# Where the memory tokens of a cross attention are loaded and turned: in the merge before w_mix_out instead of inside it

## The chip, the core and the metric

The kernel runs on one core of one Trainium2 chip. The metric is the device time of one execution in microseconds (us). The engines work side by side, each through its own instructions in order: TensorE (PE, with its weight loads as PEld), VectorE (DVE), ScalarE (ACT), GpSimd (POOL) and SyncE (SP). Transfers are issued by SP (the hardware queue) or by POOL (the software queue) and carried out by 16 DMA engines.

## The reference

One decoder block on 256 tokens of 2048 features, all in float32:

```
u = rms_norm(x);  [q k v z B C g_attn g_conv] = u @ w_in
merged = sigmoid(g_attn) * (attention(q, k, v) @ w_attn_proj)
       + sigmoid(g_conv) * (B * conv3(C * z) @ w_conv_proj)
h = x + merged @ w_mix_out
u = rms_norm(h);  mem_n = rms_norm(mem)          # mem: 256 memory tokens of 2048 features
k, v = halves of mem_n @ w_xkv;  q = u @ w_xq    # 4 heads of 128
h = h + softmax(q k^T / sqrt(128)) v @ w_xo
h = h + swiglu(rms_norm(h));  out = rms_norm(h)
```

The change concerns `rms_norm(mem)` and how its result gets into the layout that `mem_n @ w_xkv` needs: features on the 128 partitions, tokens along the free axis.

## The kernel before, in words

Every product keeps float32 accuracy by splitting both operands into a high part (rounded to fp32r) and a low part (the rest) and adding three partial products. Weights come in tiles of 256 rows by 512 columns (512 KB), loaded by SP into `raw` (five buffers). ScalarE casts a tile to `whi` and VectorE subtracts to get `wlo` (three buffers each; `split`, L54 to L56, called from `weights`, L70). `gemm_ft` (L86) makes [features, tokens]: for each weight tile a matmul of 512 columns with `whi` (L96) and one of 256 with `wlo` (L100). `gemm_tf` (L112) makes [tokens, features]: triples of matmuls of 512 columns (L122, L123, L124), where L123 alone reads `wlo`. Between weight tiles a product runs "hooks", pieces of other work given by the row number k0 at which they are traced.

The order: `w_in` in 17 products of 512 columns (the last eight make the two gates; attention runs in their hooks), then the merge (L513 to L535), then `w_mix_out` (L576 to L588), then the cross attention and the feed-forward part. The merge has eight `gemm_ft` products, `w_attn_proj` and `w_conv_proj` in turn for each of four column blocks, of four weight tiles each. What they leave is gated, added and split into MG. `w_mix_out` has four `gemm_tf` products of eight weight tiles each, with MG as the other operand. Its results are added to `h`, which holds a copy of x that POOL loads at L577.

An activation is transposed without TensorE as follows. `stage_in` (L225) loads a block so that partition 32 i + b holds tokens 32 j + b and the i-th quarter of its columns. `feat` (L208) then transposes its 32 x 32 squares on VectorE (L214, into `xt`, two buffers, two 128 x 256 pieces in each) and calls `high_low` (L217), where ScalarE multiplies by the gain (L221) and VectorE makes the low part (L222). Before the change mem is staged as one tile of [128, 8, 512] in the tile pool `cp`, by four POOL transfers of 512 KB in the first two products of `w_mix_out` (L578 to L580). It is turned by eight calls of `mem_feat` in the last two (L582, L583), and its norm is taken from the staged tile by `stage_rms` (L229, called at L587). The result is XM, the operand of `w_xkv`. The residual h is staged per column block by `bounce` (L249): SP writes the block to DRAM (`hd`, L252) and reads it back in the staged layout (`hst`, four transfers, L227). `h_feat` (L570) turns it, traced as hooks of the two products of `w_xkv` that follow.

Each engine's order is written by a planner when the program is built. It runs a model of the machine's time and gives an engine the next instruction that is ready in that model, the earlier traced first; an instruction can so stand well ahead of its place in the program. `keep_in_program_order` pins an instruction behind the one that was traced before it on its engine. A tile needs a free buffer of its pool, and a pool opened in the room of a closed one waits until that one's tiles are no longer used. `ap` and `cp` are such pools: `h` and `mem` lie where the mixer's tiles were, so their loads start when the merge is over.

Of the kernel before, what the change touches and what calls it, by code (L numbers as in the profile page):

```python
# [17 lines left out]
P = 128  # L18
# [23 lines left out]
def hybrid_block(ctx, tc, a, out):  # L42
# [69 lines left out]
    def gemm_tf(W, kt, X, c0, evac, cols=C, hooks=None, last=1, lead=0, head=1):  # L112
        """[tokens, features] tiles of X.T @ W[:, c0:c0+cols]; the first and last weight tiles go token tile by token tile."""
# [50 lines left out]
    # keep the tensor engine's clock up while the first loads are under way  # L164
# [4 lines left out]
    # additive masks: current block keeps key <= query, previous block key > query  # L169
# [11 lines left out]
    def sumsq(src, ss):  # L181
        junk = sp.tile([P, C], F32, tag="junk", name="junk", bufs=1)
        nc.scalar.activation(junk, src, AF.Square, accum_out=ss)
# [14 lines left out]
    # A staged block holds 32 i + b on its partitions, for token 32 j + b and features (i, f):  # L198
    # transposing its 32 x 32 squares puts features on the partitions and tokens next to each other.
# [8 lines left out]
    def feat(stage, m, k0, n, kx, g, X, j0=0, nj=NJ):  # L208
        """X[:, kx + k, 0/1, tokens] = high/low parts of (stage * g) for the features f = m a + k0 + k."""
# [3 lines left out]
        for k in range(n):  # L213
            nc.vector.transpose(xt[:, k, :].rearrange("p (j b) -> p j b", b=Q), v[:, k0 + k, j0:j0 + nj, :])  # L214
# [14 lines left out]
    def stage_rms(stage, name):  # L229
        """1/rms of the tokens of a staged block: [P, NT] by partition, and [P, T] on every partition."""  # L230
# [18 lines left out]
    def bounce(c, st, eng=nc.sync):  # L249
        """Stage column chunk c of h by way of DRAM."""  # L250
# [5 lines left out]
    def spread(r, name):  # L256
        """rB[p, t*P + n] = r[n, t] on every partition p."""
# [12 lines left out]
    # ================= mixer =================  # L270
    with ExitStack() as ph:
        mp = ph.enter_context(tc.tile_pool(name="mp", bufs=1))
        ap_ = ph.enter_context(tc.tile_pool(name="ap", bufs=2))
# [17 lines left out]
        k_sb = mp.tile([P, NT, KVW], F32, tag="k_sb", name="k_sb")  # L291
        v_sb = mp.tile([P, NT, KVW], F32, tag="v_sb", name="v_sb")
# [20 lines left out]
        g_x, g_mem, g_ffn = gain("g_xattn", C // P), gain("g_mem", KD), gain("g_ffn", C // P)  # L313
# [10 lines left out]
        # rotary, in place, on GpSimd  # L324
# [20 lines left out]
        # gated short convolution, [features, tokens]  # L345
        yc = mp.tile([P, KC, 2, T], F32R, tag="yc", name="yc")
        for c in range(CW // C):
            zts = []

            def evac_z(m, p0, p1, zts=zts):  # L350
                if not zts:
                    zts.append(mp.tile([P, C // P, T], F32, tag="zt", name="zt"))
# [8 lines left out]
            def evac_c(m, p0, p1, c=c, zts=zts):  # L361
                zt = zts[0]
                cz = mp.tile([P, T + 2], F32, tag="cz", name="cz", bufs=4)
# [26 lines left out]
        # attention stages per kv head  # L390
        qT = mp.tile([P, NH // 2, T], F32, tag="qT", name="qT")
        kT = mp.tile([P, 2, NKV // 2, T], F32, tag="kT", name="kT")
        ks_sb = mp.tile([P, NT, KVW], F32, tag="ks_sb", name="ks_sb")
# [103 lines left out]
        }  # L497
        i = 0
        for dst, base in ((sa, AW + 2 * KVW + 3 * CW), (sc, AW + 2 * KVW + 3 * CW + D)):
            for c in range(D // C):  # L500
                hooks = {4 * j + 2: [f] for j, f in enumerate(steps.get(i, ()))}
                i += 1

# [9 lines left out]
        # merge  # L513
        MG = xp.tile([P, KD, 2, T], F32R, tag="X", name="MG")
        for c in range(D // C):
# [16 lines left out]
            gemm_ft(rows_kp(a["w_attn_proj"][0]), AW // P, oT, c * C, evac_a)  # L532
            gemm_ft(rows_kp(a["w_conv_proj"][0]), KC, yc, c * C, evac_m)
        while pending:
            next(pending.pop(0), None)  # L535

# [15 lines left out]
    # ================= cross attention =================  # L552
    with ExitStack() as ph:
        cp = ph.enter_context(tc.tile_pool(name="cp", bufs=1))
        cap = ph.enter_context(tc.tile_pool(name="cap", bufs=2))
        mem = cp.tile([P, NJ, C], F32, tag="mem", name="mem")
        xv = a["x"][0].rearrange("(t p) d -> p t d", p=P)

        XM = cp.tile([P, KD, 2, T], F32R, tag="XM", name="XM")
# [4 lines left out]
        rm, hs = [], {}  # L564

# [7 lines left out]
        def mem_feat(k):  # L573
            feat(mem, KD, k, 2, k, g_mem, XM)

        for c in range(D // C):  # L576
            hooks = {4: [lambda: nc.gpsimd.dma_start(h[:, :, c * C:(c + 1) * C], xv[:, :, c * C:(c + 1) * C])]}  # L577
            if c < 2:  # L578
                hooks[8] = [lambda: stage_in(mem, a["mem"][0], 2 * c, eng=nc.gpsimd)]
                hooks[12] = [lambda: stage_in(mem, a["mem"][0], 2 * c + 1, eng=nc.gpsimd)]  # L580
            else:
                for i in range(4):  # L582
                    hooks[2 + 4 * i] = [lambda i=i: mem_feat((c - 2) * KD // 2 + 2 * i)]  # L583
            if c:
                hooks[4].append(lambda: h_stage(c - 1))
            if c == D // C - 1:
                hooks[4].append(lambda: rm.extend(stage_rms(mem, "rmB")))  # L587
# [3 lines left out]
        xs = cp.tile([P, NJ * C], F32, tag="mem", name="xs")  # L591
# [12 lines left out]
        gemm_ft(rows_pk(a["w_xkv"][0], KD), KD, XM, 0, evac_xk, hooks=hooks)  # L604
# [13 lines left out]
        gemm_tf(rows_pk(a["w_xkv"][0], KD), KD, XM, XW, evac_xv(0), cols=HW, hooks=hooks)  # L618
# [168 lines left out]
```

## Time and profile before

| | us |
|---|---|
| median of 3 runs | 1473.47 |
| lowest, highest | 1473.1, 1473.87 |
| span of the profiled execution | 1474.0 |
| TensorE busy in it | 1441.9 |
| VectorE busy | 886.3 |
| ScalarE busy | 724.0 |
| mean granted clock of TensorE | 0.991 |

The profiled execution's own time is its span, 1474.0 us; the profile shows nothing outside it. Positions such as 545.20 are microseconds from the start of the span. Matmuls are pipelined: a duration of 0.39 us is from start to end, and the next one starts 0.23 us after it.

### The profile page before, as it was taken

The numbers are of one execution on the slowest core, as the hardware profiler recorded it, in microseconds if no ns is written. First come the engines' busy times: TensorE is split into PE (matmuls) and PEld (weight loads), VectorE is DVE, ScalarE is ACT, GpSimd is POOL, SyncE is SP. The second block draws the span as 40 slices with busy tenths as digits, with TensorE's granted clock in tenths as the row PEclk, the third lists the DMA queues.
The fourth block names the chain that finished last, engine by engine and source line by source line (L and its number), as shares of the span: only waits on it lengthen the run. The fifth ranks groups of instructions, "written<-read, shape, count | busy, mean of one in ns | idle before, by whom it ended". The sixth has DMA issues, their size and how long they took to land.

```text
span 1474.0 us, 20189 instructions
## 1 busy us (share of the span) xinstructions
PE 1441.9 (98%) x7707; PEld 1227.6 (83%) x7707; DVE 886.3 (60%) x1316; ACT 724.0 (49%) x1115; POOL 46.6 (3%) x67
## 2 busy tenths in 40 slices
PE   7999999999999996999999999999999999999997
PEld 6888888888888875899888888888888888888886
DVE  6557768555557858585655656556556555545454
ACT  6443555554455545565654544545445444434343
POOL 0061000000000010000000000000000000000000
PEclk9999999999999998999999999999999999999999
DMA  8664454456656678865566665665666666555553
GB/s 227 198 188 147 145 170 148 155 176 198 191 176 192 194 204 241 254 192 163 175 186 186 186 195 183 194 188 186 193 190 184 190 193 217 187 188 189 191 188 115
DMA packets 147028, 275.11 MB, mean 187 GB/s; under 512 B 10588, under 2 KB 18804, under 8 KB 146804
## 3 DMA queue, kind: packets, MB, share of 16 engines
q1 hardware_dynamic: 145780, 269.64, 59.3%
q0 software_dynamic: 1152, 4.19, 1.2%
q8 instruction: 60, 0.98, 0.3%
q14 instruction: 36, 0.29, 0.1%
HBM read 269.60 MB, written 4.19 MB: 186 GB/s over the span
## 4 chain that ended last, share of the span: by engine, by line
PE 92%; DMA 2%; POOL 2%; DVE 2%; issue 1%; ACT 0%; ACTq 0%; POOLq 0%; SPq 0%; DVEq 0%
PE acc L96 41%; PE acc L100 21%; PE acc L123 9%; PE acc L124 9%; PE acc L122 9%; DMA mem<-in_mem 2%; DMA x<-in_x 1%; DVE xt L214 1%; PE sps L430 1%; PE ops L483 1%; DVE XM L222 0%; DVE wlo L56 0%; PE tp L472 0%; POOL sa L336 0%; POOL sa L335 0%
## 5 line engine op out<-in xcount | busy, mean ns | idle before, releaser
L56 DVE TENSOR_TENSOR wlo<-raw,whi 128x1024 fp32r<-128x1024 f32 (+1 forms) x506 | 607.0, 1205 | 527.1 <-ACT whi L55 526.9
L55 ACT CAST whi<-raw 128x1024 fp32r<-128x1024 f32 (+1 forms) x506 | 520.2, 1033 | 624.5 <-PE acc L96 359.7
L96 PE MATMUL acc<-X,whi 128*128 128x512 f32 x2368 | 805.8, 396 | 0.0
L100 PE MATMUL acc<-X,wlo 128*128 128x256 f32 x2368 | 607.3, 280 | 0.0
L96 PEld LDWEIGHTS acc<-X,whi 128*128 128x128 f32 x2368 | 435.9, 188 | 83.6 <-issue 0.8
L100 PEld LDWEIGHTS acc<-X,wlo 128*128 128x128 f32 x2368 | 446.2, 188 | 23.9 <-issue 1.1
L124 PE MATMUL acc<-whi,gT 128*128 128x512 f32 x352 | 138.9, 395 | 0.0
L123 PE MATMUL acc<-wlo,gT 128*128 128x512 f32 x352 | 138.9, 394 | 0.0
L122 PE MATMUL acc<-whi,gT 128*128 128x512 f32 x352 | 125.4, 395 | 0.0
L107 ACT COPY half<-acc 128x256 f32<-128x256 f32 x184 | 67.5, 369 | 25.5 <-PE acc L100 23.5
L122 PEld LDWEIGHTS acc<-whi,gT 128*128 128x128 f32 x352 | 66.4, 189 | 15.5
L124 PEld LDWEIGHTS acc<-whi,gT 128*128 128x128 f32 x352 | 66.3, 188 | 15.5
L123 PEld LDWEIGHTS acc<-wlo,gT 128*128 128x128 f32 x352 | 66.3, 188 | 15.4
L123 PE MATMUL acc<-wlo,MG 128*128 128x512 f32 x128 | 51.0, 399 | 12.7 <-DVE wlo L56 12.7
L124 PE MATMUL acc<-whi,MG 128*128 128x512 f32 x128 | 50.6, 395 | 0.0
L122 PE MATMUL acc<-whi,MG 128*128 128x512 f32 x128 | 45.4, 393 | 0.0
L96 PE MATMUL acc<-yc,whi 128*128 128x512 f32 x128 | 43.7, 394 | 0.0
L96 PE MATMUL acc<-oT,whi 128*128 128x512 f32 x128 | 43.5, 394 | 0.0
L122 PE MATMUL acc<-whi,X 128*128 128x512 f32 x96 | 34.4, 401 | 5.9 <-ACT whi L55 3.3
L123 PEld LDWEIGHTS acc<-wlo,MG 128*128 128x128 f32 x128 | 24.5, 192 | 18.7 <-DVE wlo L56 13.5
L123 PE MATMUL acc<-wlo,X 128*128 128x512 f32 x96 | 38.2, 403 | 0.9 <-DVE wlo L56 0.9
L124 PE MATMUL acc<-whi,X 128*128 128x512 f32 x96 | 37.6, 397 | 0.0
(189 smaller groups left out, 1106.1 us busy)
## 6 DMA issues: line engine op xcount, KB each, us to landing
raw<-in_w_ffn_in SPq DMA_DIRECT2D x176, 512.0 KB, 4.3
raw<-in_w_in SPq DMA_DIRECT2D x134, 512.0 KB, 3.8
raw<-in_w_ffn_out SPq DMA_DIRECT2D x88, 512.0 KB, 4.6
raw<-in_w_mix_out SPq DMA_DIRECT2D x32, 512.0 KB, 4.8
raw<-in_w_attn_proj SPq DMA_DIRECT2D x16, 512.0 KB, 4.3
raw<-in_w_conv_proj SPq DMA_DIRECT2D x16, 512.0 KB, 4.0
raw<-in_w_xkv SPq DMA_DIRECT2D x8, 512.0 KB, 3.9
raw<-in_w_xkv SPq DMA_DIRECT2D x16, 256.0 KB, 2.8
```

The costliest lines, as they stand in the source:

```text
L55: nc.scalar.copy(hi, src)
L56: nc.vector.tensor_tensor(out=lo, in0=src, in1=hi.bitcast(F32), op=ALU.subtract)
L96: nc.tensor.matmul(ps[m], lhsT=hi[:, k, ms], rhs=X[:, kk].rearrange("p s t -> p (s t)"), start=(kk == 0), stop=False,)
L100: nc.tensor.matmul(ps[m][:, :T], lhsT=lo[:, k, ms], rhs=X[:, kk, 0, :], start=False, stop=(kk == kt - 1),)
L107: nc.scalar.copy(t2, ps[m][:, T:])
L122: nc.tensor.matmul(o, lhsT=xh, rhs=hi[:, k, :cols], start=(kk == 0), stop=False)
L123: nc.tensor.matmul(o, lhsT=xh, rhs=lo[:, k, :cols], start=False, stop=False)
L124: nc.tensor.matmul(o, lhsT=xl, rhs=hi[:, k, :cols], start=False, stop=(kk == kt - 1))
L214: nc.vector.transpose(xt[:, k, :].rearrange("p (j b) -> p j b", b=Q), v[:, k0 + k, j0:j0 + nj, :])
L430: nc.tensor.matmul(sps[par][:, j].rearrange("p a b -> p (a b)"), lhsT=qT[b:b + 64, hh // 2, t * P:(t + 1) * P], rhs=kT[b:b + 64, sw, kv // ...
L483: nc.tensor.matmul(ops[64 * par:64 * par + 64], lhsT=v_sb[:, kb, vs], rhs=pt[:, t + kb, par::2, :], start=(kb == 0), stop=(kb == t),)
```

## The change

The attention's pool `ap` moves to the right end of the memory and takes in the tiles that only the attention and the convolution use. It is closed before the last gate product, and two pools open in its room: `xm` with XM, and `ms` for staging. Mem is now staged in four column chunks of 512 features, each a tile `mst` of [128, 8, 128] filled by four POOL transfers of 128 KB (512-byte runs). A second copy, in natural layout, comes in eight tiles `mnat` of [128, 512] (256 KB) for the sums of squares. Both have two buffers. Chunks 0 and 1 and natural tiles 0 and 1 are loaded in hooks of the last gate product, the others in the merge. In the merge's first four products (g = 0 to 3) chunk g is turned by two calls of `feat`, whose first transpose is pinned; in each of the eight products one natural tile is squared and summed on ScalarE, pinned as well. The norm comes from these sums (`mem_rms`) with no matmul. Features lie in XM in another order now, so `g_mem` and the rows of `w_xkv` are read in that order too (`rows_pk(..., C // P)`). In `w_mix_out` the loads, the turns and `stage_rms` of mem go. Removed comments and docstrings, and unchanged context, are left out here:

```diff
-    def feat(stage, m, k0, n, kx, g, X, j0=0, nj=NJ):
+    def feat(stage, m, k0, n, kx, g, X, j0=0, nj=NJ, late=False):
         ...
         for k in range(n):
-            nc.vector.transpose(xt[:, k, :].rearrange("p (j b) -> p j b", b=Q), v[:, k0 + k, j0:j0 + nj, :])
+            i = nc.vector.transpose(xt[:, k, :].rearrange("p (j b) -> p j b", b=Q), v[:, k0 + k, j0:j0 + nj, :])
+            if late and not k:
+                tc.keep_in_program_order(i)
...
+    mxp, ms = ExitStack(), ExitStack()
     with ExitStack() as ph:
         mp = ph.enter_context(tc.tile_pool(name="mp", bufs=1))
-        ap_ = ph.enter_context(tc.tile_pool(name="ap", bufs=2))
+        at = ph.enter_context(ExitStack())
+        ap_ = at.enter_context(tc.tile_pool(name="ap", bufs=2, side="right"))
...
         # k_sb, v_sb, zt, cz, qT, kT, ks_sb: from mp to ap_, with the same number of buffers
-        g_x, g_mem, g_ffn = gain("g_xattn", C // P), gain("g_mem", KD), gain("g_ffn", C // P)
+        g_x, g_mem, g_ffn = (gain(n, C // P) for n in ("g_xattn", "g_mem", "g_ffn"))
...
+        mem_in, mem_do = {}, {}
+
+        def mem_open():
+            at.close()
+            xm = mxp.enter_context(tc.tile_pool(name="xm", bufs=1, side="right"))
+            tmp = ms.enter_context(tc.tile_pool(name="ms", bufs=2, side="right"))
+            XM = xm.tile([P, KD, 2, T], F32R, tag="XM", name="XM")
+            ssm = tiny.tile([P, NT, D // C], F32, tag="ssm", name="ssm")
+            mv = a["mem"][0].rearrange("(t p) d -> p t d", p=P)
+
+            def stage(c):
+                mem_in[c] = tmp.tile([P, NJ, P], F32, tag="mst", name="mst")
+                for i in range(P // Q):
+                    stage_in(mem_in[c], a["mem"][0][:, c * C:(c + 1) * C], i, eng=nc.gpsimd)
+
+            def turn(c, k):
+                feat(mem_in[c], C // P, k, 2, c * (C // P) + k, g_mem, XM, late=True)
+
+            def nat(j):
+                mem_in[4 + j] = tmp.tile([P, C], F32, tag="mnat", name="mnat")
+                c, t = j // NT, j % NT
+                nc.gpsimd.dma_start(mem_in[4 + j], mv[:, t, c * C:(c + 1) * C])
+
+            def sums(j):
+                c, t = j // NT, j % NT
+                tc.keep_in_program_order(sumsq(mem_in[4 + j], ssm[:, t, c:c + 1]))
...
                 i += 1
+                if i == 8:
+                    mem_open()
+                    do = mem_do
+                    hooks = {0: [lambda: do["stage"](0)], 2: [lambda: do["stage"](1)],
+                             4: [lambda: do["nat"](0)], 6: [lambda: do["nat"](1)]}
...
+            def mem_hooks(g):
+                hk = {2: [lambda: do["sums"](g)], 4: []}
+                if g < 6:
+                    hk[2].append(lambda: do["nat"](g + 2))
+                if g < 4:
+                    hk[2].append(lambda: do["turn"](g, 0))
+                    hk[4].append(lambda: do["turn"](g, 2))
+                    if g < 2:
+                        hk[4].append(lambda: do["stage"](g + 2))
+                return hk
+
-            gemm_ft(rows_kp(a["w_attn_proj"][0]), AW // P, oT, c * C, evac_a)
-            gemm_ft(rows_kp(a["w_conv_proj"][0]), KC, yc, c * C, evac_m)
+            gemm_ft(rows_kp(a["w_attn_proj"][0]), AW // P, oT, c * C, evac_a, hooks=mem_hooks(2 * c))
+            gemm_ft(rows_kp(a["w_conv_proj"][0]), KC, yc, c * C, evac_m, hooks=mem_hooks(2 * c + 1))
         while pending:
             next(pending.pop(0), None)
+        ms.close()
...
-        mem = cp.tile([P, NJ, C], F32, tag="mem", name="mem")
+        ph.enter_context(mxp)
+        XM = mem_do["XM"]
...
+        def mem_rms():
+            r = rstd_sum(mem_do["ssm"])
+            rm.extend((r, spread(r, "rmB")))
...
-            if c < 2:
-                hooks[8] = [lambda: stage_in(mem, a["mem"][0], 2 * c, eng=nc.gpsimd)]
-                hooks[12] = [lambda: stage_in(mem, a["mem"][0], 2 * c + 1, eng=nc.gpsimd)]
-            else:
-                for i in range(4):
-                    hooks[2 + 4 * i] = [lambda i=i: mem_feat((c - 2) * KD // 2 + 2 * i)]
...
-                hooks[4].append(lambda: rm.extend(stage_rms(mem, "rmB")))
+                hooks[4].append(mem_rms)
...
-        gemm_ft(rows_pk(a["w_xkv"][0], KD), KD, XM, 0, evac_xk, hooks=hooks)
+        gemm_ft(rows_pk(a["w_xkv"][0], C // P), KD, XM, 0, evac_xk, hooks=hooks)
```

## Rows read from the trace of the kernel before

**Rows 1.** The page: TensorE's busy time, and the chain's shares by line.

```profile
PE 1441.9 (98%) x7707; PEld 1227.6 (83%) x7707; DVE 886.3 (60%) x1316; ACT 724.0 (49%) x1115; POOL 46.6 (3%) x67
PE acc L96 41%; PE acc L100 21%; PE acc L123 9%; PE acc L124 9%; PE acc L122 9%; DMA mem<-in_mem 2%; DMA x<-in_x 1%; DVE xt L214 1%; PE sps L430 1%; PE ops L483 1%; DVE XM L222 0%; DVE wlo L56 0%; PE tp L472 0%; POOL sa L336 0%; POOL sa L335 0%
```

**Rows 2.** TensorE's waits, 515 to 650 us: total, times, longest.

```profile
PE acc L123 <- DVE wlo L56: 12.7, 2, 11.5
```

**Rows 3.** VectorE's order of time: start, us, line, out<-in, count, [idle before].

```profile
545.20 0.68 DVE L541 TENSOR_TENSOR h<-acc,h 128x512 f32<-128x512 f32 x1
559.29 2.08 DVE L214 STREAM_TRANSPOSE xt<-mem 128x256 f32<-128x256 f32 x4 [13.41 <-DMA mem<-in_mem]
...
561.87 1.21 DVE L56 TENSOR_TENSOR wlo<-raw,whi 128x1024 fp32r<-128x1024 f32 x1
...
583.98 2.21 DVE L214 STREAM_TRANSPOSE xt<-hst 128x256 f32<-128x256 f32 x4
```

**Rows 4.** TensorE's order of time: merge's start, w_mix_out's start, stop and end.

```profile
433.82 0.39 PE L96 MATMUL acc<-oT,whi 128*128 128x512 f32 x1
...
523.92 0.39 PE L123 MATMUL acc<-wlo,MG 128*128 128x512 f32 x1
...
550.93 0.71 PE L122 MATMUL acc<-whi,MG 128*128 128x512 f32 x2
563.13 0.80 PE L123 MATMUL acc<-wlo,MG 128*128 128x512 f32 x1 [11.49 <-DVE wlo L56]
...
626.20 0.62 PE L96 MATMUL acc<-XM,whi 128*128 128x512 f32 x2
```

**Rows 5.** VectorE's order of time in the third product of w_mix_out.

```profile
591.64 1.22 DVE L56 TENSOR_TENSOR wlo<-raw,whi 128x1024 fp32r<-128x1024 f32 x1 [1.47 <-ACT whi L55]
...
597.08 1.23 DVE L56 TENSOR_TENSOR wlo<-raw,whi 128x1024 fp32r<-128x1024 f32 x1 [1.50 <-ACT whi L55]
```

**Rows 6.** Windows: length, PE, PEld, DVE, ACT, POOL busy, granted clock, DMA, GB/s.

```profile
554.00:556.00 2.00, 0.00 (x0) 0.00 (x0) 0.00 (x0) 0.00 (x0) 0.00 (x0) 1.00 1.04 223
556.00:558.00 2.00, 0.00 (x0) 0.00 (x0) 0.00 (x0) 0.00 (x0) 0.00 (x0) 0.57 1.02 297
...
564.00:566.00 2.00, 2.00 (x6) 1.52 (x6) 2.00 (x5) 0.78 (x2) 0.00 (x0) 0.50 0.88 257
```

**Rows 7.** POOL's order of time, 530 to 626 us: its first instruction there.

```profile
532.01 0.91 POOL L577 DMA_DIRECT2D h<-in_x  x1 [414.06 <-issue]
```

**Rows 8.** DMA queues from 544 to 556 us: packets, MB, share of the engines.

```profile
q0 software_dynamic: 508, 1.85, 65.1%
q1 hardware_dynamic: 506, 0.97, 39.0%
```

**Rows 9.** Windows, the merge's eight products: the third, and the sum of all.

```profile
456.28:467.51 11.23, 11.23 (x66) 9.81 (x65) 10.10 (x21) 6.95 (x12) 0.00 (x0) 1.00 0.59 187
...
sum 89.86, PE 89.86 PEld 78.52 DVE 68.02 ACT 49.23 POOL 0.00; mean PE 11.23 PEld 9.82 DVE 8.50 ACT 6.15 POOL 0.00
```

**Rows 10.** ScalarE's order of time, 540 to 592 us.

```profile
549.80 1.05 ACT L55 CAST whi<-raw 128x1024 fp32r<-128x1024 f32 x1 [5.78 <-DMA raw<-in_w_mix_out]
```

**Rows 11.** DMA issues 530 to 565 (KB, us to landing); hst 585 to 600.

```profile
hd<-h SPq DMA_DIRECT2D x1, 512.0 KB, 4.3
...
DMA to landing us min/median/max: 6.7/7.2/7.5
```

**Rows 12.** VectorE by line, 524 to 626 (busy, mean ns, idle); mem's tile.

```profile
L214 DVE STREAM_TRANSPOSE xt<-mem 128x256 f32<-128x256 f32 x16 | 8.6, 582 | 13.4 <-DMA mem<-in_mem 13.4
L222 DVE SCALAR_TENSOR_TENSOR XM<-xt,g_mem,XM 128x256 fp32r<-128x256 f32 x16 | 6.7, 467 | 0.0
...
DMA to landing us min/median/max: 12.5/18.2/23.8
```

**Rows 13.** VectorE's order of time in the merge's first product.

```profile
439.78 2.36 DVE L56 TENSOR_TENSOR wlo<-raw,whi 128x1024 fp32r<-128x1024 f32 x2 [2.40 <-ACT whi L55]
```

**Rows 14.** The instructions that read pt: duration min/median/max, first and last start.

```profile
L483 PE MATMUL ops<-pt,v_sb x48: 379/379/431, 175.3 to 300.3; 128*64 128x256 f32 x48
```

More of the change, by code (lines that the diff above doesn't have):

```diff
@@ L182, in sumsq @@
         junk = sp.tile([P, C], F32, tag="junk", name="junk", bufs=1)
-        nc.scalar.activation(junk, src, AF.Square, accum_out=ss)
+        return nc.scalar.activation(junk, src, AF.Square, accum_out=ss)
     def rstd_sum(ss):
@@ L290, in hybrid_block @@
         q_sb = mp.tile([P, NT, AW], F32, tag="sc", name="q_sb")
-        k_sb = mp.tile([P, NT, KVW], F32, tag="k_sb", name="k_sb")
-        v_sb = mp.tile([P, NT, KVW], F32, tag="v_sb", name="v_sb")
+        k_sb = ap_.tile([P, NT, KVW], F32, tag="k_sb", name="k_sb", bufs=1)
+        v_sb = ap_.tile([P, NT, KVW], F32, tag="v_sb", name="v_sb", bufs=1)
         def evac_q(c):
@@ L351, in evac_z @@
                 if not zts:
-                    zts.append(mp.tile([P, C // P, T], F32, tag="zt", name="zt"))
+                    zts.append(ap_.tile([P, C // P, T], F32, tag="zt", name="zt", bufs=1))
                 zt = zts[0]
@@ L362, in evac_c @@
                 zt = zts[0]
-                cz = mp.tile([P, T + 2], F32, tag="cz", name="cz", bufs=4)
+                cz = ap_.tile([P, T + 2], F32, tag="cz", name="cz", bufs=4)
                 nc.vector.memset(cz[:, 0:2], 0.0)
@@ L388, in hybrid_block @@
             gemm_ft(W, KD, X1, AW + 2 * KVW + CW + c * C, evac_b)
-        qT = mp.tile([P, NH // 2, T], F32, tag="qT", name="qT")
-        kT = mp.tile([P, 2, NKV // 2, T], F32, tag="kT", name="kT")
-        ks_sb = mp.tile([P, NT, KVW], F32, tag="ks_sb", name="ks_sb")
+        qT = ap_.tile([P, NH // 2, T], F32, tag="qT", name="qT", bufs=1)
+        kT = ap_.tile([P, 2, NKV // 2, T], F32, tag="kT", name="kT", bufs=1)
+        ks_sb = ap_.tile([P, NT, KVW], F32, tag="ks_sb", name="ks_sb", bufs=1)
         oT = mp.tile([P, AW // P, 2, T], F32R, tag="x0", name="oT")
@@ L497, in hybrid_block @@
         }
+        mem_in, mem_do = {}, {}
[19 more added lines that the diff above has]
+                tc.keep_in_program_order(sumsq(mem_in[4 + j], ssm[:, t, c:c + 1]))
+            mem_do.update(stage=stage, turn=turn, nat=nat, sums=sums, XM=XM, ssm=ssm)
         i = 0
@@ L555, in hybrid_block @@
         cap = ph.enter_context(tc.tile_pool(name="cap", bufs=2))
-        mem = cp.tile([P, NJ, C], F32, tag="mem", name="mem")
+        ph.enter_context(mxp)
+        XM = mem_do["XM"]
         xv = a["x"][0].rearrange("(t p) d -> p t d", p=P)
-        XM = cp.tile([P, KD, 2, T], F32R, tag="XM", name="XM")
         X2 = xp.tile([P, KD, 2, T], F32R, tag="X", name="X2")
@@ L571, in h_feat @@
             feat(hs[c], C // P, k, 2, c * (C // P) + k, g, X)
-        def mem_feat(k):
-            feat(mem, KD, k, 2, k, g_mem, XM)
         for c in range(D // C):
             hooks = {4: [lambda: nc.gpsimd.dma_start(h[:, :, c * C:(c + 1) * C], xv[:, :, c * C:(c + 1) * C])]}
-            if c < 2:
-                hooks[8] = [lambda: stage_in(mem, a["mem"][0], 2 * c, eng=nc.gpsimd)]
-                hooks[12] = [lambda: stage_in(mem, a["mem"][0], 2 * c + 1, eng=nc.gpsimd)]
-            else:
-                for i in range(4):
-                    hooks[2 + 4 * i] = [lambda i=i: mem_feat((c - 2) * KD // 2 + 2 * i)]
             if c:
@@ L586, in hybrid_block @@
             if c == D // C - 1:
-                hooks[4].append(lambda: rm.extend(stage_rms(mem, "rmB")))
+                hooks[4].append(mem_rms)
             gemm_tf(rows_kp(a["w_mix_out"][0]), KD, MG, c * C, residual(c, ss1), hooks=hooks)
         xkT = cp.tile([P, XH, T], F32, tag="xkT", name="xkT")
-        xs = cp.tile([P, NJ * C], F32, tag="mem", name="xs")
+        xs = cp.tile([P, NJ * C], F32, tag="xs", name="xs")
         xqT = xs[:, :XH * T].rearrange("p (h t) -> p h t", h=XH)
@@ L617, in hybrid_block @@
         hooks = {2: [lambda: h_feat(D // C - 1, 0, g_x, X2)], 6: [lambda: h_feat(D // C - 1, 2, g_x, X2)]}
-        gemm_tf(rows_pk(a["w_xkv"][0], KD), KD, XM, XW, evac_xv(0), cols=HW, hooks=hooks)
+        gemm_tf(rows_pk(a["w_xkv"][0], C // P), KD, XM, XW, evac_xv(0), cols=HW, hooks=hooks)
         gemm_ft(rows_pk(a["w_xq"][0], C // P), KD, X2, 0, evac_xq)
@@ L667, in hybrid_block @@
         hooks[14] += [lambda: xvalues(1)]
-        gemm_tf(rows_pk(a["w_xkv"][0], KD), KD, XM, XW + HW, evac_xv(1), cols=HW, hooks=hooks)
+        gemm_tf(rows_pk(a["w_xkv"][0], C // P), KD, XM, XW + HW, evac_xv(1), cols=HW, hooks=hooks)
         ss2 = tiny.tile([P, NT, D // C], F32, tag="ssc", name="ss2")
```

## The prediction

> **What bounds the kernel now.** I read the engine table and the chain of waits first: TensorE is busy for 1441.9 of 1474.0 us, and the chain that ended last is its matmuls almost throughout; the only transfers of any size on it are the memory tokens (2%) and x (1%) [rows 1]. So only the few stretches in which TensorE stands still can be won. Then the waits between 515 and 650 us: TensorE has one there, L123, the second matmul of `w_mix_out`'s triples, on `wlo`, 12.7 us, of which 11.5 in one piece [rows 2]. Last, VectorE's order of time, which shows why: between the first residual (545.20) and the next split (561.87) stand four transposes of `mem`, and the first of them waits 13.41 us for its transfer [rows 3]. VectorE works in order, so the split that TensorE needs stands behind a transfer that it doesn't need.
>
> What the stage loses: its first L123 on MG starts at 523.92, the first matmul on XM at 626.20, 102.3 us apart [rows 4]. Undisturbed, a weight tile takes 2.72 us (splits from 591.64 to 597.08, two steps) [rows 5]; 32 tiles make 87.1 us. The excess is 15.2 us: the 11.49 us before 563.13 [rows 4], 1.2 in the other wait [rows 2], and 2.5 in which TensorE was slow. That is mostly the clock: the grant is 1.00 until 556, 0.57 in 556:558 and 0.50 (1.2 GHz) in 564:566 [rows 6].
>
> **The change part by part, on the profiled execution's 1474.0 us** (0.5 us above the median of the three runs; I take the 0.5 off at the end).
>
> *The loads of mem leave the stage, and 16 transposes, 16 scaled subtractions and 16 activations with them.* With no mem transpose in VectorE's queue the stop and what followed it go: **-15.2 us**. What is late next is the subject of the next two parts.
>
> *Left in the stage: raw tiles.* From 532 us on four h loads and four mem loads are under way from POOL [rows 7]. While they run, the software queue moves 1.85 MB in 12 us and the weights' queue 0.97 MB [rows 8], 81 GB/s instead of some 187 [rows 9]. ScalarE waits 5.78 us for the raw tile that it casts at 549.80 [rows 10], and TensorE uses that tile at 550.93 [rows 4]: it was about to be held by the weights there too. With h alone, half of the 4.2 MB, the queue is free some 10 us earlier, and only this tile and the next are tight. I count that within the next part, since a stop there lets the weights catch up.
>
> *Left in the stage: h staged through DRAM.* This is what I expect to be late next. The program transposes `hst` in `w_xkv`, but the planner set the first four of these transposes at 583.98, in `w_mix_out`, when the last mem work had given the two `xt` buffers back [rows 3]. After the change `xt` is free from the start of the stage, and those four (h_feat's, which are not pinned) can stand right behind the moment at which the planner believes the first hst landed. Its belief can be early: it set mem's transposes behind 545.20, and mem came in time for 559.29 [rows 3]. The real way of the first hst: h of tile 1 is added at about 546.5; `hd` takes 4.3 us, behind up to four raw tiles issued before it; then four transfers of 6.7 to 7.5 us [rows 11]. That is 558 at the earliest, and some 8 us later if hd stands behind all the raw tiles. The bounds of the price are 0 (the planner's time is right) and 15.2 us (the same stop once more). The nearest row is the mem wait itself: 13.41 us of VectorE that became 11.49 of TensorE, a cushion of 1.9. Half of the surplus bytes are in flight, so I take half of the wait: 6.7 - 1.9 = 4.8 us, and 1.2, half of the 2.5, for the clock, since the grant had still been 1.00 when TensorE had stood for 4 us [rows 4, 6]. **+6.0 us (0 to 15.2).**
>
> *The merge.* Each of its eight products takes TensorE 11.23 us. VectorE is busy for 10.10 us in the third, fifth and seventh, and by the sum of 68.02 for 7.5 in each other one [rows 9]. The 16 transposes hold VectorE 8.6 us and the 16 subtractions 6.7 [rows 12]: 15.3 us, 3.8 in each of the first four products. That makes 11.4, 11.4, 13.9, 11.4: over the product's time by 0.2, 0.2, 2.7 and 0.2, together 3.3 us at the end of the fourth. VectorE's lead covers a part. It is shortest at a product's last weight tile: that split starts at 439.78 and takes about 1.2 us [rows 13], and TensorE, which began the product at 433.82 [rows 4], comes to the tile after three quarters of it, at 442.2: 1.2 us of lead. So TensorE stands 2.1 us if that lead decides, and not at all if the planner puts the turns where VectorE waits for ScalarE. From the fifth product on VectorE has time again (83.3 of 89.9 us in all). ScalarE gets 24 operations; at 1.05 us, its large cast [rows 10], they would be 25 us onto 49.2 of 89.9: hidden.
>
> The Trainium skill has a rule that makes this dearer ("VectorE: DVE Perf Modes", section "The DRAIN you can't avoid"): an operation does not start until the pipe behind the one before is empty. By it the two groups cost their count times their mean, 9.3 + 7.5 = 16.8 us, the overshoot is 4.8 us and the price up to 3.6. The trace does not bear it out: four transposes of 0.58 us take 2.08 together, so each starts a little before the last has ended [rows 3, 12].
>
> The pinned transposes of chunks 2 and 3 also need transfers that start only when chunks 0 and 1 have been turned: 1 3/4 products, 19.7 us, earlier. Mem's transfers took 12.5 to 23.8 us beside 4 MB of others [rows 12]; here 0.5 MB and a natural tile run beside weights that take 0.59 of the DMA engines [rows 9]. At 23.8 each wait would be 4 us. **+1.0 us for the merge (0 to 5).**
>
> *The early loads.* Two chunks and two natural tiles (1.5 MB) can start when the attention's tiles are free; the last matmul on `pt` starts at 300.3 [rows 14], 133 us before the first use. At 1.85 MB in 12 us [rows 8] they take 10 us. The contention from 532 to 549 was longer and cost TensorE nothing: 0 (0 to 2). POOL is idle for the 414 us before 532 [rows 7], so no queue is held. The gain g_mem is loaded in another order, the sums replace eight squares on ScalarE near 610, the rows of `w_xkv` are renumbered: TensorE has no wait at any of these, 0 (-0.5 to 0.5).
>
> **Sum:** 1474.0 - 15.2 + 6.0 + 1.0 = 1465.8; less 0.5 for the median, **1465.3 us**.
>
> **Rivals.** *Nothing takes the stop's place:* hst's transposes fall where the data is there. For it: no transpose of hst waited in the trace; against it: xt was never free early. 1465.3 - 6.0 = 1459.3, or 1458.3 with the merge free too.
>
> *The wait is only exchanged:* hst, two transfers in a row and behind the weights, comes as late as mem did. 15.2 instead of 6.0 gives 1474.5, no change. For it: VectorE's queue has the same order, one wait of unknown length ahead of the splits; against it: half of the surplus traffic.
>
> *Slower, the merge waits for its own chunks:* the pinned transposes of chunks 2 and 3 stand ahead of the splits. If their transfers take 19.7 + w us, TensorE stands w less 1.2, twice. With hst's 6.0 the gain is 9.2, so from w = 5.8 (25.5 us in flight) nothing is left, and from 7.3 it is slower by over 0.2%. At w = 10, and 2.5 for the clock after each stop, it costs 22.6: 1474.0 - 0.5 - 9.2 + 22.6 = 1486.9. Against it: 23.8 us is the longest transfer of mem, in far more traffic [rows 12].
>
> *It does not do what it says:* the room on the right is free only after the merge has begun, and its first transposes wait as in the last rival. Rows 14 speak against it.
>
> **How the numbers follow.** A measurement of this kernel can tell about 0.2%, 2.9 us: faster is under 1470.5, slower over 1476.4. Chances: forecast 0.43 (its own range 1462 to 1470), nothing in its place 0.29, exchanged 0.15, slower by the merge or its room 0.13. Of "exchanged" and "slower" a part ends on either side of those lines. Faster 0.76, same 0.13, slower 0.11. The range goes from 1458 (both new prices at zero) to 1472 (hst at 12 us, the merge at 1.7).
>
> **What would show it.** Right: no mem transpose in `w_mix_out` and no 11 us piece of L123 on wlo; a wait of VectorE's L214 for `hst` of 4 to 9 us between 550 and 568, with a stop of TensorE of some 5 us behind it; in the merge TensorE waits on wlo of 2 us at most, in the third and fourth product, and VectorE busy for 83 us. Wrong: the stage from MG to XM in 88.5 us or less (hst costs nothing), a stop of over 10 us in it (exchanged), or a wait for `mst` in the merge.

## The result, and the profile after

The changed kernel takes **1455.35 us** (median of 4 runs, 1454.2 to 1456.41); the kernel before, on the same chip, 1473.67 us (1473.1 to 1476.33). The ratio is 0.9869, with a 95% interval of 0.9855 to 0.9883: 18.3 us faster. The forecast was 1465.3 us with a range of 1458 to 1472, so it had the sign and missed the size: the time lies below the range. The profiled execution of after has a span of 1452.4 us and a time of 1454.2 us: the time is longer than the span by 1.7 to 2.1 us in every run of this study, so the profiled execution of before, with its span of 1474.0 us, took about 1476 us.

I cut both traces at the same instructions: the first matmul on `oT` (merge), the first L123 on MG (`w_mix_out`), the first matmul on XM (cross attention), on `xo` (`w_xo`), on X behind it (feed-forward in) and on `gT` (feed-forward out).

| us | before | after | after less before |
|---|---|---|---|
| start to merge | 433.82 | 431.96 | -1.9 |
| merge | 90.10 | 91.95 | +1.85 |
| `w_mix_out` | 102.28 | 87.33 | -14.95 |
| cross attention | 74.87 | 74.67 | -0.2 |
| `w_xo` | 25.87 | 25.50 | -0.4 |
| feed-forward in | 492.56 | 492.57 | 0 |
| feed-forward out, to the end | 254.48 | 248.46 | -6.0 |
| span | 1474.0 | 1452.4 | -21.6 |

The stage that was edited did what the forecast said of its old wait. Two rows of this table are not in the forecast: 6.0 us in the last product, some 500 us behind the last edited line, and 1.9 us at the start.

Of the page of after, the engine table and the chain by line, against [rows 1]: VectorE, ScalarE and the number of matmuls are nearly as before, TensorE is busy for 9.6 us less, and no transfer of mem is on the chain.

```profile
PE 1432.3 (99%) x7705; PEld 1223.9 (84%) x7705; DVE 885.5 (61%) x1314; ACT 722.7 (50%) x1115; POOL 59.1 (4%) x87
PE acc L96 42%; PE acc L100 21%; PE acc L123 10%; PE acc L122 10%; PE acc L124 10%; DMA x<-in_x 1%; PE sps L434 1%; PE ops L487 1%; PE tp L476 0%; POOL sa L339 0%; POOL sa L340 0%; POOL sa L342 0%; PE tp L722 0%; DMA raw<-in_w_mix_out 0%; PE sps L679 0%
```

VectorE's order of time in `w_mix_out` of after, against [rows 3] (start, us, line, out<-in, count, [idle before]). No mem transpose is left. The transposes of `hst` have come forward, as forecast, and the first of them waits for its transfer, but for 3.10 us and not for 13.41:

```profile
552.19 1.22 DVE L56 TENSOR_TENSOR wlo<-raw,whi 128x1024 fp32r<-128x1024 f32 x1 [1.50 <-ACT whi L55]
556.51 2.21 DVE L214 STREAM_TRANSPOSE xt<-hst 128x256 f32<-128x256 f32 x4 [3.10 <-DMA hst<-hd]
558.63 3.46 DVE L56 TENSOR_TENSOR wlo<-raw,whi 128x1024 fp32r<-128x1024 f32 x3
```

TensorE's order of time in after, against [rows 4]: the merge's start, the stage's start, the one wait in it, and its end. Behind VectorE's 3.10 us of waiting and 2.21 of transposes TensorE stands for 0.20 us:

```profile
431.96 0.39 PE L96 MATMUL acc<-oT,whi 128*128 128x512 f32 x1
...
523.91 0.39 PE L123 MATMUL acc<-wlo,MG 128*128 128x512 f32 x1
...
559.88 0.50 PE L123 MATMUL acc<-wlo,MG 128*128 128x512 f32 x1 [0.20 <-DVE wlo L56]
...
611.24 0.62 PE L96 MATMUL acc<-XM,whi 128*128 128x512 f32 x2
```

The transfers of after: the queues from 529 to 541 us (packets, MB, share of the engines), against [rows 8], which are as long; then, from the list of issues, the first `hst` (KB, us to landing), against [rows 11]:

```profile
q0 software_dynamic: 566, 2.07, 52.0%
q1 hardware_dynamic: 800, 1.54, 33.8%
...
hst<-hd SPq DMA_DIRECT2D x4, 128.0 KB, 3.4
```

The weights' queue moves 1.54 MB in the time in which it moved 0.97. A packet of it takes 81 ns of an engine (33.8% of 16 x 12 us over 800) against 148 in [rows 8], one of the software queue 176 against 246. [Rows 8] are from the middle of the loads of before; the like stretch is its first 12 us of loads, 532 to 544 us:

```profile
q0 software_dynamic: 410, 1.53, 61.0%
q1 hardware_dynamic: 611, 1.19, 35.6%
```

There the weights' queue had 1.19 MB and 112 ns for a packet: against like, it is 1.3 times as fast in after. The h loads land after 4.8 to 11.1 us, where they took 9.4 to 26.4 beside mem.

TensorE in the merge of after (order of time): the only two waits, 1.02 us together, both in the fourth product.

```profile
467.87 0.39 PE L100 MATMUL acc<-yc,wlo 128*128 128x256 f32 x1 [0.81 <-DVE wlo L56]
...
469.05 0.50 PE L96 MATMUL acc<-yc,whi 128*128 128x512 f32 x1 [0.21 <-DVE s L141]
```

The windows of the same stage, against [rows 9] (length, then busy time of PE, PEld, DVE, ACT and POOL, granted clock, DMA share, GB/s): the third and fourth product's stretches, and the sum of all. VectorE is full in the third, and TensorE stands in the fourth.

```profile
454.42:465.65 11.23, 11.23 (x64) 9.51 (x64) 11.23 (x25) 7.96 (x17) 0.56 (x1) 1.00 0.63 210
465.65:476.88 11.23, 10.21 (x57) 8.41 (x56) 10.36 (x21) 6.55 (x12) 0.55 (x1) 1.00 0.56 193
...
sum 91.95, PE 90.93 PEld 78.71 DVE 80.89 ACT 58.91 POOL 8.20; mean PE 11.37 PEld 9.84 DVE 10.11 ACT 7.36 POOL 1.03
```

The last product, by line and operand (count, busy us, mean ns of one, idle before), in the kernel before:

```profile
L124 PE MATMUL acc<-whi,gT 128*128 128x512 f32 x352 | 138.9, 395 | 0.0
L123 PE MATMUL acc<-wlo,gT 128*128 128x512 f32 x352 | 138.9, 394 | 0.0
```

and in the kernel after:

```profile
L124 PE MATMUL acc<-whi,gT 128*128 128x512 f32 x352 | 136.9, 389 | 0.0
L123 PE MATMUL acc<-wlo,gT 128*128 128x512 f32 x352 | 136.9, 389 | 0.0
```

TensorE waits for nothing in either. The same 1056 matmuls simply follow each other faster: 6.0 us over 1056 is 5.7 ns for each, and from start to start the median goes from 232 to 227 ns.

### The profile page after: what moved, and what is told of

It is laid out like the page before. It is cut to its first block, busy times and chain, and to the rows that moved or that the text cites. A ratio compares the mean times of both kernels' runs of the same rounds, so it can differ in the third digit from the quotient of the medians.

```text
span 1452.4 us, 20222 instructions
## 1 busy us (share of the span) xinstructions
PE 1432.3 (99%) x7705; PEld 1223.9 (84%) x7705; DVE 885.5 (61%) x1314; ACT 722.7 (50%) x1115; POOL 59.1 (4%) x87
## 4 chain that ended last, share of the span: by engine, by line
PE 95%; POOL 2%; DMA 1%; issue 1%; DVE 0%; ACT 0%; ACTq 0%; POOLq 0%; SPq 0%; DVEq 0%
PE acc L96 42%; PE acc L100 21%; PE acc L123 10%; PE acc L122 10%; PE acc L124 10%; DMA x<-in_x 1%; PE sps L434 1%; PE ops L487 1%; PE tp L476 0%; POOL sa L339 0%; POOL sa L340 0%; POOL sa L342 0%; PE tp L722 0%; DMA raw<-in_w_mix_out 0%; PE sps L679 0%
## 5 line engine op out<-in xcount | busy, mean ns | idle before, releaser
L96 PE MATMUL acc<-X,whi 128*128 128x512 f32 x2368 | 804.3, 395 | 0.0
L100 PE MATMUL acc<-X,wlo 128*128 128x256 f32 x2368 | 606.7, 280 | 0.0
L96 PEld LDWEIGHTS acc<-X,whi 128*128 128x128 f32 x2368 | 435.2, 188 | 83.2 <-issue 0.8
L100 PEld LDWEIGHTS acc<-X,wlo 128*128 128x128 f32 x2368 | 445.5, 188 | 23.9 <-issue 1.1
L124 PE MATMUL acc<-whi,gT 128*128 128x512 f32 x352 | 136.9, 389 | 0.0
L123 PE MATMUL acc<-wlo,gT 128*128 128x512 f32 x352 | 136.9, 389 | 0.0
L122 PE MATMUL acc<-whi,gT 128*128 128x512 f32 x352 | 123.5, 389 | 0.0
L123 PEld LDWEIGHTS acc<-wlo,gT 128*128 128x128 f32 x352 | 66.1, 188 | 13.7
L123 PE MATMUL acc<-wlo,MG 128*128 128x512 f32 x128 | 49.9, 390 | 0.2 <-DVE wlo L56 0.2
L195 POOL TENSOR_TENSOR rstd<-ms,mhalf 128x2 f32<-128x2 f32 (+1 forms) x6 | 6.1, 1024 | 967.6 <-DVE ms L193 967.6
L96 PE MATMUL acc<-yc,whi 128*128 128x512 f32 x128 | 44.1, 397 | 0.2 <-DVE s L141 0.2
L96 PE MATMUL acc<-oT,whi 128*128 128x512 f32 x128 | 43.7, 395 | 0.0
L123 PE MATMUL acc<-wlo,X 128*128 128x512 f32 x96 | 38.7, 408 | 0.0
```

The costliest lines, as they stand in the source:

```text
L96: nc.tensor.matmul(ps[m], lhsT=hi[:, k, ms], rhs=X[:, kk].rearrange("p s t -> p (s t)"), start=(kk == 0), stop=False,)
L100: nc.tensor.matmul(ps[m][:, :T], lhsT=lo[:, k, ms], rhs=X[:, kk, 0, :], start=False, stop=(kk == kt - 1),)
L122: nc.tensor.matmul(o, lhsT=xh, rhs=hi[:, k, :cols], start=(kk == 0), stop=False)
L123: nc.tensor.matmul(o, lhsT=xh, rhs=lo[:, k, :cols], start=False, stop=False)
L124: nc.tensor.matmul(o, lhsT=xl, rhs=hi[:, k, :cols], start=False, stop=(kk == kt - 1))
L195: nc.gpsimd.tensor_tensor(out=r, in0=ms, in1=mhalf[:, :n], op=ALU.pow)
```

## The experiments

All kernels but one, the repeat of after, are edits of before or of after by a few lines. "Stage" is a row of the table above, in the profiled execution.

**Is the last product's gain an accident of an address?** In the built programs `gT` begins at byte 133,984 of each partition before and at 134,112 after. The change's new small tile `ssm` (four buffers of 32 bytes) pushed it up by 128 bytes; `whi` and `wlo`, from 75,488 on, did not move. So the address is moved alone, in before:

```diff
+    pad = tiny.tile([P, 8], F32, tag="pad", name="pad")
+    nc.gpsimd.memset(pad, 0.0)
```

> The kernel before with one tiny tile more (four buffers of 32 bytes per partition), so that everything behind that pool, gT among it, lies 128 bytes higher, as the change's own small tile ssm moved it; all the work is the same. In the two traces w_ffn_out takes 254.5 us before and 248.5 after, its matmuls running at 131 against 134 in 30 us, although nothing in that stage was edited. Theory A (the place of gT in the memory sets the pace): w_ffn_out takes 248 to 249 us, and the total is some 6 to 7.5 us under the kernel before, 1466 to 1468. Rival B (the pace comes from something else that the change altered earlier, or from the run): w_ffn_out stays at 254 to 255, and the total within 1.5 us of before.

Measured: 1463.68 us (1462.91 to 1465.36) against 1473.89, ratio 0.9933 (0.9918 to 0.9948); last product 248.47 us. And moved back, in after, with the small tile under a tag whose room was there already:

```diff
-            ssm = tiny.tile([P, NT, D // C], F32, tag="ssm", name="ssm")
+            ssm = tiny.tile([P, NT, D // C], F32, tag="ssj", name="ssm")
```

> The changed kernel with ssm put into a tag that is there already, so that gT and h lie where they did before the change. Theory A (place of gT): w_ffn_out goes back to 254 to 255 us and the total to 1461 to 1463, 6 to 7 us over the changed kernel. Rival B: w_ffn_out stays at 248 to 249 and the total at 1454 to 1457. This run also says what the change is worth without the accident of the address: by theory A about 12 us of the 18.

Measured: 1462.03 us (1460.95 to 1463.95) against 1473.89, ratio 0.9922 (0.9907 to 0.9937); last product 254.46 us. The address carries the 6.0 us in both directions, and the change without it is worth 11.9 us. The windows from 1310 to 1340 us show the pace with TensorE busy all the time: 134 matmuls in 30 us in the shifted before,

```profile
1310.00:1340.00 30.00, 30.00 (x134) 24.86 (x133) 16.08 (x16) 12.95 (x15) 0.00 (x0) 1.00 0.63 194
```

and 131 in after with `gT` put back:

```profile
1310.00:1340.00 30.00, 30.00 (x131) 24.34 (x130) 16.01 (x15) 12.37 (x15) 0.00 (x0) 1.00 0.60 192
```

The first of the two gained more than 6 us: the loads of h and mem began at 528.14 instead of 532.01, that is 6.05 us after the start of their stage instead of 8.09, and the stop in `w_mix_out` was 3.6 us on `wlo` and 2.6 on `whi` (stage 97.66). That was not foreseen, and it is no part of the last product's 6.0 us. Why the loads began earlier stays open: but for the added memset the order of the instructions on each engine is the same in the two traces.

**What about the address?** Three kernels, one run each: after with 128 bytes put ahead of every tile but the few at the right end (`gT` and the weights move together), and after with 64 or 256 bytes ahead of `gT` alone.

```diff
+    pad = const.tile([P, 32], F32, name="pad")
+    nc.gpsimd.memset(pad, 0.0)
```

> The changed kernel with 128 bytes put at the very front of the memory, so that every tile on the left (weights, X, MG, gT, xo) lies 128 bytes higher; the distances between them stay. Two earlier runs showed that gT at 134112 gives 248.5 to 249 us in w_ffn_out and gT at 133984 gives 254 to 255, with the weights at 75488 and 87776 in both. Theory H (the distance between the two operands of a matmul decides): w_ffn_out stays at 248 to 249 us and the feed-forward's first part at 518, the total within 2 us of the changed kernel. Rival I (the address itself decides): w_ffn_out goes to 254 or 255, and the other products, whose operands now lie at such places too, slow down by about 1 to 2.5% as well: the total is 1467 to 1475.

Measured: last product 248.46 us, 1455.09 in all. Then, at the place where `gT` is allocated, 64 bytes as here, and 256 bytes with `[P, 64]`:

```diff
+        pad = fp.tile([P, 16], F32, tag="pad", name="pad")
+        nc.gpsimd.memset(pad, 0.0)
```

> The changed kernel with gT alone 64 bytes higher (134176). From gT to the weights' tiles the distance is then 64 more than a multiple of 256; it was a multiple of 256 in the changed kernel (fast) and 128 off one in the kernel before (slow). Theory H1 (only a whole multiple of 256 is fast): w_ffn_out takes 252 to 256 us. Rival H2 (only the 128 bytes matter, 64 do not): it stays at 248 to 249.

> The changed kernel with gT alone 256 bytes higher (134368), so that its distance to the weights' tiles is again a multiple of 256 (of 512 too, where it was 256 off one). Theory H1 (multiples of 256 are fast): w_ffn_out stays at 248 to 249 us. Rival H3 (the 512 bytes of a row matter, or the pace was tied to the one address): it changes by more than 1 us.

Measured: with 64 bytes 255.48 us (1462.58 in all), with 256 bytes 248.45 (1456.29). The windows with 64 bytes, where start to start is 233 ns:

```profile
1310.00:1340.00 30.00, 30.00 (x131) 24.02 (x130) 16.00 (x15) 12.07 (x16) 0.00 (x0) 1.00 0.60 191
```

and with 256:

```profile
1310.00:1340.00 30.00, 30.00 (x134) 24.84 (x133) 16.00 (x15) 13.03 (x16) 0.00 (x0) 1.00 0.61 193
```

Fast is a distance between `gT` and `whi` that is a multiple of 256 bytes (58,624 in after, the same with everything moved, 58,880 with 256 bytes more); slow are 58,496 (before) and 58,688 (64 more). The absolute address does not decide. `raw`, `whi` and `wlo` lie at multiples of 512 bytes from each other in all these kernels, so it is not shown which of them counts. Distances of other kinds were not tried, and why it is so stays open.

**What of the 15 us in `w_mix_out` was VectorE's order, what the traffic?** Before, with mem's transposes pinned where they are traced, so that none can stand ahead of a split; first only the first of each pair, as the change does it, then both, with `if late:` (the transpose's operands and the new parameter are left out here):

```diff
+            i = nc.vector.transpose(...)
+            if late and not k:
+                tc.keep_in_program_order(i)
...
+            feat(mem, KD, k, 2, k, g_mem, XM, late=True)
```

> The kernel before with the first transpose of each mem pair pinned behind what was traced before it on VectorE; mem is loaded in the same place as before. Theory C (the stop was only the order: a transpose that the planner set too early ahead of the splits): the 11.5 us stop goes, w_mix_out takes 87.5 to 91 us and the total is 1459 to 1463. Rival D (the stop was in part the traffic: the raw tiles landed at 549.7, about 556 and 561 while TensorE needed them at about 548.8, 551.5 and 554.2): with the order mended TensorE still stops for ScalarE's casts, 5 to 7 us in all between 550 and 562, w_mix_out takes 92 to 97 and the total is 1464 to 1469.

Measured: 1473.2 us, ratio 0.9992 (0.9983 to 1.0002); stage 99.92. Neither theory: one second transpose, not pinned, went ahead alone and waited just as long. VectorE's order of time in that kernel:

```profile
545.35 0.68 DVE L543 TENSOR_TENSOR h<-acc,h 128x512 f32<-128x512 f32 x1
559.87 0.60 DVE L214 STREAM_TRANSPOSE xt<-mem 128x256 f32<-128x256 f32 x1 [13.83 <-DMA mem<-in_mem]
560.40 0.65 DVE L543 TENSOR_TENSOR h<-acc,h 128x512 f32<-128x512 f32 x1
560.97 1.21 DVE L56 TENSOR_TENSOR wlo<-raw,whi 128x1024 fp32r<-128x1024 f32 x1
```

With both pinned:

> As the run with the first transpose of each mem pair pinned, with both pinned: there one unpinned transpose was left ahead of the second residual, and VectorE waited 13.83 us for mem as before. Now no mem transpose can stand in VectorE's queue before the third product. Theory C (the stop was only VectorE's order): w_mix_out takes 87.5 to 91 us, the total is 1459 to 1463. Rival D (the traffic of mem and h together holds the weights as well): in the run before this the raw tiles landed at 550.6, 557.3 and 561.8, where TensorE needs a tile every 2.72 us from 551; TensorE then waits for ScalarE's casts, 5 to 7 us in all between 551 and 563, w_mix_out takes 92 to 97 us and the total is 1464 to 1469.

Measured: 1467.8 us (1466.08 to 1468.44) against 1474.68, ratio 0.9955 (0.9938 to 0.9972); stage 92.49. The stop of 11.5 us is gone, and the raw tiles are late in its place. ScalarE's order of time there:

```profile
549.28 1.05 ACT L55 CAST whi<-raw 128x1024 fp32r<-128x1024 f32 x1 [5.28 <-DMA raw<-in_w_mix_out]
...
555.43 1.04 ACT L55 CAST whi<-raw 128x1024 fp32r<-128x1024 f32 x1 [3.72 <-DMA raw<-in_w_mix_out]
559.45 1.05 ACT L55 CAST whi<-raw 128x1024 fp32r<-128x1024 f32 x1 [2.98 <-DMA raw<-in_w_mix_out]
```

and TensorE's waits from 515 to 640 us (total, times, longest):

```profile
PE acc L122 <- ACT whi L55: 2.5, 2, 2.3
PE acc L123 <- DVE wlo L56: 1.1, 2, 0.5
```

Rival D's stage and total came true; the waits that it put at 5 to 7 us are 3.6 in this list, and with the slower matmuls around them all of the 5.2 us over 87.33 lie between 551 and 562, but for 0.2. So mem cost the stage twice: by its place in VectorE's order, and by its bytes beside h and the weights. The change takes both away; a pin takes only the first. The split is not sharp. In the profiled executions the order is 9.8 of the 15 us and the bytes 5.2; by the medians of the timed runs the pin is worth 6.9, which leaves 8. The profiled execution of the pinned kernel was the fastest of its four, and its grant stayed at 1.00 from 548 to 566, through these waits, where it fell to 0.50 in before [rows 6]; the mean clock of the other three runs is 0.993 against its 0.995. That the grant fell in those is likely, but not shown.

**What does the merge cost?** After, with the eight turns of mem spread over all eight products in place of the first four:

```diff
-                if g < 4:
-                    hk[2].append(lambda: do["turn"](g, 0))
-                    hk[4].append(lambda: do["turn"](g, 2))
-                    if g < 2:
-                        hk[4].append(lambda: do["stage"](g + 2))
+                hk[2].append(lambda: do["turn"](g // 2, g % 2 * 2))
+                if g in (1, 3):
+                    hk[4].append(lambda: do["stage"](g // 2 + 2))
```

> The changed kernel with the eight turns of mem spread over the merge's eight products, one in each, instead of two in each of the first four. In the changed kernel the merge takes 91.9 us against 90.1 before, and TensorE waits there 0.8 and 0.2 us on VectorE in the fourth product. Theory E (the 1.8 us are VectorE's overload in the first four products): the merge takes 90.0 to 90.6 us and the total is 1.3 to 1.9 us under the changed kernel, 1453 to 1454. Rival F (the merge is longer through something else, such as the addresses or the transfers): the merge stays at 91.5 to 92.2 and the total is unchanged. Rival G (the overload only moves to the third, fifth and seventh product): waits of 0.5 to 1 us on wlo appear in these.

Measured: 1453.78 us (1452.79 to 1454.6) against 1473.89, ratio 0.9866 (0.985 to 0.9883); merge 90.01 us, as long as before, with no wait of TensorE in it. That is theory E. The windows of its fourth product and of the whole stage, where after had 10.21 and 90.93 us of PE:

```profile
465.90:477.15 11.25, 11.25 (x67) 9.85 (x66) 9.88 (x18) 7.19 (x14) 1.83 (x4) 1.00 1.00 224
...
sum 90.01, PE 90.01 PEld 78.68 DVE 80.55 ACT 57.64 POOL 8.25; mean PE 11.25 PEld 9.83 DVE 10.07 ACT 7.21 POOL 1.03
```

**Is VectorE's wait for hst worth anything?** The spread turns again, with both transposes of each pair pinned, those of h too (`if late:`, and `late=True` in `h_feat`); and after itself once more on the same chip.

> The kernel after with the eight turns spread over the eight products of the merge, as in e4_after_spread, and with both transposes of each pair pinned to the place where they are written, those of h and those of the memory tokens. What the early transposes of h cost as the next thing late was 0.2 us of TensorE's waiting in the kernel after, though VectorE stood 3.1 us for them. Theory P (a wait on VectorE that TensorE does not feel is worth nothing): VectorE's 3.1 us for hst go, mix_out stays at 87.0 to 87.7 us, the whole at 1453 to 1455 us, as e4_after_spread. Rival Q (VectorE's order in mix_out still costs something that the list of waits doesn't show): mix_out falls to 85.5 to 86.5 us and the whole to 1452 or under. Rival R (transposes pinned late stand in the way of the cross-attention): mix_out as now, but the cross-attention's stage grows from 74.7 us by 1 us or more, the whole 1455 to 1457 us.

> The kernel after, unedited, on the same chip, so that the two stand side by side: 1454 to 1456.5 us. If spreading the turns is worth its stage's 1.9 us, e7_spread_pinh stands 1 to 2 us below it; if the stage's gain is given back elsewhere, they are within 0.7 us.

Measured: 1454.01 us (1452.73 to 1454.46) and 1454.8 us (1454.34 to 1455.69) against 1475.67; ratios 0.9852 (0.9837 to 0.9866) and 0.9859 (0.9843 to 0.9876). Pinned, the first transpose of `hst` starts at 610.3 instead of 556.5 and VectorE waits for no `hst`; the stage takes 86.84 us, after's repeat 86.87. VectorE's wait was 2.55 us in that repeat, and worth nothing. It isn't so in every execution. In the traces of after and of its variants with the same order, VectorE waits for `hst` and TensorE behind it for `wlo`: 2.55 and 0 us, 2.79 and 0, 3.10 and 0.20, 3.39 and 0.5, 3.61 and 0.7, 3.98 and 1.1, 4.10 and 1.2. From 2.9 us on TensorE pays what goes beyond, so this wait costs 0 to 1.2 us. With the pins the cross attention is 0.8 us longer (75.47 against 74.67). The transposes of `hst` now all stand there, and that they cost it is likely; the list of TensorE's waits names none of it. The spread's 1.8 us are in the merge again (90.15 against 91.95). In all the two kernels are not told apart: 1.8 less in the merge, 0.8 more in the cross attention, 0.5 more at the start. Nor do the totals show that the spread without the pins is faster than after: it is 20.1 us under its before, after is 18.3 under its own the first time and 20.9 the second (ratios 0.9866, 0.9869 and 0.9859). For it speaks the merge's stage alone, 1.9 us shorter, in one profiled execution of it and one of the kernel with the pins.

## Why the prediction was wrong, step by step

**The premise failed: "So only the few stretches in which TensorE stands still can be won."** 6.0 us were won in a stretch in which it never stands still, before or after. A busy TensorE was read as a TensorE at its pace. The trace of before had the sign of it: matmuls of one shape take 232 ns from start to start on `gT` and 227 on MG. 6.0 of the 10 us by which the forecast missed are this, and no term, rival or bound had a place for it. (The distance of `xo` to the weights went from 128 bytes off a multiple of 256 to such a multiple as well, and its matmuls from 232 to 227 ns: the 0.4 us of `w_xo`, 25.50 in the shifted before too and 25.84 with the address put back.)

**The term of hst was mis-sized: +6.0 us, measured 0.2.** (It is 0 to 1.2 in the traces with the same order.) The mechanism was right to the place (VectorE's L214 waiting for `hst` between 550 and 568, 3.10 us where 4 to 9 were forecast). What failed is "Half of the surplus bytes are in flight, so I take half of the wait". The `hst` transfers landed after 3.4 us, where the forecast took 6.7 to 7.5. That row is of the second column block, issued at 589.8 us; the first four `hst` transfers in the trace of before, issued at 569.8, had taken 5.2 to 5.5. By then mem had landed, so that mem's bytes made them slow is not shown. With mem gone the weights' queue was faster (1.54 MB against 1.19 in the first 12 us of the loads), and the splits ahead were done early. The cushion was larger too: 3.10 us of VectorE's waiting became 0.20 of TensorE's, 2.9 us, not 1.9. The rival "nothing takes the stop's place", with 0.29, was the true case in this stage, and the forecast's own sign of it came: the stage took less than 88.5 us. Its 1459.3 us, less the 6.0 of the address, is 1453.3, near the measured 1455.35.

**The stop itself: -15.2 forecast, -14.95 measured**, with hst's 0.2 in it. Its two causes, order and traffic, were both named; the forecast left the raw tiles without a price, and rightly: with mem gone ScalarE's lateness no longer reaches TensorE.

**The merge: +1.0 (0 to 5) forecast, +1.85 measured.** The step was right in kind: VectorE over its limit in the third product, and TensorE held at the fourth, for want of `wlo`. The size is near the 2.1 that the lead of 1.2 us gave; I had taken half. It is nearer than it looks, for the new addresses of `oT` and `yc` hide a part: with the addresses put back the merge takes 92.22 us, 2.1 over before, and the shifted before, which has the new addresses and no turns, takes 89.49. VectorE's sum is 80.89 us where 83.3 were forecast; four of the sixteen transposes of mem (307.48, 428.72, 429.27 and 431.49) start ahead of the merge. The Trainium skill's rule of the drained pipe ("VectorE: DVE Perf Modes", section "The DRAIN you can't avoid"), by which the price would have been up to 3.6 us, is not borne out here either: the four transposes of the row at 556.51 take 0.60 to 0.65 us each and 2.21 together. The same section adds that an operation that is not held starts earlier; the prediction left that out, and with it the page and the trace do not contradict each other. No wait for `mst` or a natural tile is found in the merge, so the rival "the merge waits for its own chunks" fell.

**The early loads: 0 forecast, 0 measured for TensorE.** POOL's order of time in after: eight `mst` loads go at 299.49, when the attention's tiles are free, and TensorE never waits for one; VectorE stands 2.1 us for `mst`, far ahead of any use, and POOL's own queue 1.6.

```profile
299.49 4.82 POOL L229 DMA_DIRECT2D mst<-in_mem  x8 [180.78 <-ACT oT L55]
304.30 0.59 POOL L524 DMA_DIRECT2D mnat<-in_mem  x1
306.49 0.56 POOL L524 DMA_DIRECT2D mnat<-in_mem  x1 [1.60 <-DMA mst<-in_mem]
```

**The start: nothing forecast, -1.9 in the profiles.** It is not the change: the same program as after took 433.11 us to the merge when run again, 1.15 more than the first time, and the kernels of this study lie between 431.96 and 434.26 there. Most of it is the clock, below. The profiled execution of before was also a long one: with the 1.8 to 2.1 us outside its span it took about 1476 us, more than 2 above the median of its runs, where I took off 0.5. This is why the spans differ by 21.6 us and the medians by 18.3. The terms that the runs bear out, -14.95, -6.0 and +1.85, make -19.1, within the interval of the ratio (-17.2 to -21.4).

## What to carry to other kernels

A wait's price is not halved with its bytes: with mem's loads gone the next transfer took 3.4 us in place of 5.2 to 7.5, and the lead in front of the wait was 2.9 us in place of 1.9, so price the next wait from a stretch without that traffic, and subtract the lead. Before calling a busy engine's stretches fixed, compare the start-to-start time of one shape of instruction across its operands; a pace that differs is time that any new tile can win or lose by moving an address. And run the change once with the old addresses, or its gain is credited to the wrong edit.

## What the runs showed of the hardware

The pace of a 512-column fp32r matmul hung on the distance in the partition between the stationary operand (`gT`) and the weights' tiles, which hold the moving one: 227 ns at multiples of 256 bytes, 232 and 233 at 128 and 64 bytes off them, 6 to 7 us over the 1056 matmuls of the last product. The triples on `xo` do the same. In the pairs of `gemm_ft`, where the weights are the stationary operand, less hangs on it: in the merge L100 takes 120 ns from start to start with `oT` 128 bytes off such a multiple (before, and after with the address put back) and 117 at one (after, and the shifted before), and the stage goes from 90.10 to 89.49 us by the shift alone. L96 takes 232 ns on X, also at a multiple, so 227 is no rule for every order of matmuls.

The granted clock differs from run to run behind the same stop. TensorE stands for 2 us from 110 on. In before the grant then falls to 0.64 (windows as above),

```profile
112.00:114.00 2.00, 2.00 (x9) 1.77 (x10) 2.00 (x3) 0.00 (x0) 2.00 (x2) 0.64 0.00 0
```

and in the repeat of after it stays at 1.00:

```profile
110.00:112.00 2.00, 0.00 (x0) 0.00 (x0) 2.00 (x4) 0.00 (x0) 1.92 (x4) 1.00 0.44 170
112.00:114.00 2.00, 1.99 (x13) 1.81 (x14) 2.00 (x3) 0.00 (x0) 2.00 (x2) 1.00 0.00 0
```

Five of the twelve profiled executions have the fall and seven have not, whichever kernel it was. With it the merge begins at 433.61 to 434.26 us, without it at 431.96 to 433.11: about 1.4 us of this kernel's time that no edit explains.
